# Holding side products back in the plan of a two-layer decoder trunk on one core

## The chip, the core and the metric

The kernel runs on one core of a Trainium2 chip. What counts is the device time of one execution in microseconds (us). Before the change three runs gave 1103.56, 1106.44 and 1106.52 us, the median is 1106.44. The engines are named PE (TensorE), ACT (ScalarE), DVE (VectorE), POOL (GpSimd) and SP (SyncE); SP and POOL also issue the DMAs.

## What is computed

Two layers of a decoder trunk take 256 prompt tokens and 8 sample tokens (264 columns) of width 2048. In each layer the input is normalised and projected by `w_in` into 57 column tiles of 128, three branches work on parts of that, each branch is multiplied by a gate, and `w_out` brings the 2048 mixed channels back:

```
h = rms_norm(x, norm_w)
z = h @ w_in
y_a = rwkv_time_mix(z_a, ...)      # 12 heads x 64, delta-rule state, one step a token
y_b = attention_branch(z_b, ...)   # 12 heads x 64 in 3 groups, windows 128/512/2048, dilation 1/4/16
y_c = pool_branch(z_c, ...)        # causal means over 2, 4, 8, 16 tokens, then a linear map
y = x + concat(y_a, y_b, y_c) @ w_out
```

New states, the last rows and the new keys and values are outputs too.

## The kernel before

**Stream and side products.** The two projections are the stream. Weights come in as `raw` tiles of 512 KB (`load`, 512 rows by 256 columns); ACT rounds each into `hi`, DVE writes the rest into `lo`, and PE multiplies `hi` by `xh`, `hi` by `xl` and `lo` by `xh`, the two halves of the input (in `w_out` by `mh`/`ml`, `mb` and `mc`, the halves of the mixed channels). Every stream matmul has 264 columns and adds into a PSUM bank of the tag `acc` (3 banks). All else that PE does are side products: transposes (`tr`, L118), small fp32 matmuls and a few of the rounded type (`mm`, L115). They write into PSUM banks of the tag `a` (5 banks), which ACT or DVE empties.

**What a layer does in order.** `layer` projects the tiles in pairs and hands each `z` to a branch. The A branch (`a_lora`, `a_k`, `a_kdone`, `a_r`, `a_solve`, `a_v`, `a_chain`) shifts tokens, builds Gram matrices of 64-token chunks, inverts triangular ones (`invert`, four products), goes through four chunks in sequence (`chunk`, four PE bundles each: with `gs`, with `rt`, with `bt`, and the output one with `gs` and `ar`) and normalises (`group_norm`, transposes of `ots`). Its tiles live in the pool `apool`. The pool `lpool` of `late` opens once `apool` is empty. There `b_prompt` does the banded attention of the prompt (scores, softmax, transposes, values), `b_sample` that of the 8 sample tokens against the caches (`rows`, `sc`, `sml`, `sev`, `ssm`, then for each of three groups `vc`, `ex`, `os`, `osb`), `c_u` the pooling. `b_mix` multiplies by the gates and writes `mb`. Then `w_out` runs; its first weights are multiplied by four `mb` channels (order 2, 1, 3, 0).

**The plan.** Written so, the program is only a set of instructions with dependences. `Plan` gives each a rough duration (`cost`), finds who needs whom (`dependences`), and `once` goes through time like a simulation: for each engine it takes the ready instruction of the highest priority and so writes the order in which that engine runs its instructions on the chip. Each engine then runs its list strictly in order and waits on semaphores where an operand isn't there. Priority (`prio`) is the longest tail of work behind an instruction (`tails`), and the first `lead` = 25 stream matmuls and what stands before them keep program order.

The parts of `once` that matter here:

- An instruction becomes ready when the planned ends of all whom it needs have passed, plus a fixed hop between engines (`HOP`), plus `slack` of the one that waits if the two stand on different engines or the first is a DMA. `slack` is `margin` for all, and 0 for stream matmuls and what feeds them.
- A PSUM or SBUF buffer is free again 100 to 150 ns behind the planned end of its last reader (`release`); `slack` isn't added there.
- PE has two heaps, stream (`PE`) and side products (`SIDE`). If a side product is ready and `go` holds, it is taken. `go` holds if a side product was the last taken (`side_on`), if the oldest has been ready for `wait`, or if the durations of those in the heap reach `batch`. If no stream matmul is ready a side product is taken anyway.
- Going from side products back to the stream is charged `switch` = 105 ns, the other way half of it for those that aren't in a bundle (`claims`).
- Products within `with self.bundle(...)` go one after another without a break (`forced`); only the first of a bundle stands in the heap.

Of the kernel before, what the change touches and what calls it, by code (L numbers as in the profile page):

```python
# [103 lines left out]
class Trunk:  # L104
# [1185 lines left out]
    def run(self):  # L1290
        self.setup()
        with self.tc.tile_pool(name="init", bufs=1, reuse_waits="tile") as ip:
            self.ip, self.early, self.xin = ip, [], []
            calm = ip.tile([P, T], F32, name="calm")
            self.nc.vector.memset(calm, 0.0)
            pt = self.ps("a")
            calmr = ip.tile([P, 512], F32R, name="calmr")
            self.nc.vector.memset(calmr.bitcast(F32), 0.0)
            for _ in range(8):
                self.mm(pt[:, :T], calm[:, :P], calm)  # L1300
            pu = self.ps("a")
            for n, outs, rows in ((T, (pt,), (slice(0, P),)), (T, (pt, pu), (slice(0, P),)), (256, (pt,), (slice(0, P),)),
                                  (512, (pu,), (slice(0, P),)), (P, (pt,), (slice(0, P),)), (T, (pt, pu), UROWS)):
                for i in range(5):
                    r = rows[i % len(rows)]
                    self.mm(outs[i % len(outs)][:, :n], calmr[r, :P], calmr[r, :n])
            self.act(ip.tile([P, 1], F32, name="table"), calm[:, 0:1], AF.Tanh)
            self.params(0)
            for c in range(4):
                x = ip.tile([P, 4, T], F32, tag="xin", name=self.nm("xin"), bufs=4)  # L1310
                self.dma(x, self.ins["x_cm"][4 * c:4 * c + 4].rearrange("k p t -> p k t"))
                self.xin.append(x)
                if c < 3:
                    self.early.append(self.load(self.ins["w_in"][0], 23 * P, 2 * P, c))
            self.accs = self.stream(self.ins["w_in"][0], 23 * P, 2, None, None, begin=True)
            self.dma(self.cbase, self.ins["cbase"])
            self.first_scale()
            self.more_params(0)
        for l in range(self.depth):
            self.layer(l)  # L1320
# [15 lines left out]
class Plan:  # L1336
# [200 lines left out]
                tail[q] = max(tail[q], t)  # L1537
        return tail

    def run(self, factor=1, hop=300, margin=200, batch=0, wait=0, switch=0, quiet=0, lead=1, dyn=(), ahead=0):  # L1540

        self.hold = [0.0] * self.n
        args = factor, hop, margin, batch, wait, switch, quiet, lead, dyn
        if ahead:
            self.once(*args)
            for k, i in enumerate(self.ins):
                if self.dma[k] and not self.feeds(k):
                    self.hold[k] = max(0.0, min([self.start[q] for q in self.after_load[k]], default=0.0) - ahead)
        return self.once(*args)
# [1 line left out]
    def feeds(self, k):  # L1551
        return self.tag[self.first_out[k]].startswith("raw") if self.first_out[k] in self.tag else False

    def once(self, factor, hop, margin, batch, wait, switch, quiet, lead, dyn):
        n, eng, preds, dma, dur, stream = self.n, self.eng, self.preds, self.dma, self.dur, self.stream
        spare = {t: d for t, r in self.ring.items() for m, d in dyn if t.split("_" + self.pool[r[0]])[0] == m}
        tail = self.tails(factor, hop, spare)
        head = [k for k in range(n) if stream[k]][lead - 1]
        prio = [k - 3e9 if k < head else -tail[k] for k in range(n)]
        feeds = {q for k in range(n) if stream[k] for q in preds[k]}  # L1560
        slack = [0 if stream[k] or k in feeds else margin for k in range(n)]
        bust = [self.bus(i) if d else 0 for i, d in zip(self.ins, dma)]
        succ = [[] for _ in range(n)]
        count = [0] * n
# [51 lines left out]
        def take(h):  # L1616
            while h:
                p, k = heapq.heappop(h)
                w = blocked(k)
                if w is None:  # L1620
                    return k
                parked[w].append(k)
            return None
# [5 lines left out]
        while done < n:  # L1629
            while pending and pending[0][0] <= now + 1e-9:  # L1630
                _, k = heapq.heappop(pending)
# [8 lines left out]
            for e in free:  # L1640
                if free[e] > now + 1e-9 or (e == "SP" and hw > now + 700):
                    continue
                if e == "PE" and forced is not None:
                    k = forced
                elif e == "PE":
# [3 lines left out]
                    k = None  # L1649
                    if h:  # L1650
                        go = side_on or h[0][0] < -2e9 or now - since >= wait or sum(dur[x[1]] for x in h) >= batch
                        if go:
                            k = take(h)
# [3 lines left out]
                    if k is None:  # L1657
                        k = take(ready["PE"])
                        if k is None and h:
                            k = take(h)  # L1660
# [3 lines left out]
                else:  # L1664
                    k = take(ready[e])
# [134 lines left out]
def build(nc, shapes, depth=DEPTH):  # L1800
    ins = {n: nc.dram_tensor(f"in_{n}", s, F32, kind="ExternalInput").ap() for n, s in shapes.items()}
    outs = {n: nc.dram_tensor(f"out_{n}", s, F32, kind="ExternalOutput").ap() for n, s in _OUTS}
    with tile.TileContext(nc, schedule_with_timeline_sim=True) as tc, ExitStack() as ctx:
        trunk = Trunk(ctx, tc, ins, outs, depth)
        trunk.run()
        plan = Plan(tc, trunk.bundles)
        plan.run(ahead=12000, switch=105, margin=350, hop=180, factor=0.9, lead=25, quiet=60, dyn=[("a", 2)])
        plan.apply()


# [10 lines left out]
```

## Time and profile before

| | before |
|---|---|
| median of three runs | 1106.44 us |
| the profiled execution | 1103.8 us |
| its span, first to last instruction | 1102.0 us |
| mean granted TensorE clock | 0.982 of 2.4 GHz |
| busy: PE, DVE, ACT, POOL | 1053.9, 857.2, 546.1, 133.6 us |
| stream of layer 0: `w_in`, `w_out` | 11 to 458 us, 458 to 551 us |
| stream of layer 1: `w_in`, `w_out` | 551 to 1005 us, 1005 to 1099 us |

A row of the timeline gives start and duration in us, engine, line, operation, the tiles (written, then read), the shapes, and how many instructions were merged; in brackets the idle time before and who ended it. Matmuls overlap, so a matmul's duration is longer than its distance to the next; distances are taken from start to start. A row of waits says who waited for whom, for how long in sum, how often, and the longest. In a table of stretches each row gives a stretch, its length and each engine's busy time with its number of instructions, then the granted clock and the DMA engines' share and rate.

### The profile page before, as it was taken

The numbers are of one execution on the slowest core, as the hardware profiler recorded it, in microseconds if no ns is written. First come the engines' busy times: TensorE is split into PE (matmuls) and PEld (weight loads), VectorE is DVE, ScalarE is ACT, GpSimd is POOL, SyncE is SP. The second block draws the span as 40 slices with busy tenths as digits, with TensorE's granted clock in tenths as the row PEclk, the third lists the DMA queues.
The fourth block names the chain that finished last, engine by engine and source line by source line (L and its number), as shares of the span: only waits on it lengthen the run. The fifth ranks groups of instructions, "written<-read, shape, count | busy, mean of one in ns | idle before, by whom it ended". The sixth has DMA issues, their size and how long they took to land.

```text
span 1102.0 us, 24574 instructions
## 1 busy us (share of the span) xinstructions
PE 1053.9 (96%) x9802; PEld 1004.4 (91%) x9802; DVE 857.2 (78%) x1684; ACT 546.1 (50%) x934; POOL 133.6 (12%) x262
## 2 busy tenths in 40 slices
PE   9999998989999998999999999989899998999998
PEld 8999898978999887999999988988899988879998
DVE  7769968979998887666675898768899869886443
ACT  7646433445645554454464563443466553744332
POOL 0004200200022100010010141001001111000000
PEclk9999999989999999999999999989999989999999
DMA  8654578886368855677765446878864568555774
GB/s 275 209 166 135 151 232 234 243 225 208 116 209 256 267 188 174 197 225 223 231 216 169 154 136 207 226 228 212 230 196 138 172 216 307 167 187 187 226 226 151
DMA packets 154683, 223.64 MB, mean 203 GB/s; under 512 B 75984, under 2 KB 109152, under 8 KB 154552
## 3 DMA queue, kind: packets, MB, share of 16 engines
q1 hardware_dynamic: 146456, 195.94, 58.7%
q0 software_dynamic: 8112, 26.12, 7.2%
q8 instruction: 77, 1.26, 0.5%
q14 instruction: 38, 0.31, 0.1%
HBM read 198.55 MB, written 24.03 MB: 202 GB/s over the span
## 4 chain that ended last, share of the span: by engine, by line
PE 58%; DVE 19%; DMA 12%; issue 5%; ACT 4%; SPq 1%; POOL 0%; DVEq 0%; ACTq 0%; POOLq 0%
PE acc L323 50%; DVE lo L140 6%; PE a L115 5%; DMA raw<-in_w_in 5%; PE a L118 2%; ACT hi L137 2%; DVE s L140 1%; DMA qb<-q_dram 1%; DVE z L140 1%; DMA vc<-in_cache_v_w 1%; SPq L155 1%; DVE bk L149 1%; DMA iv<-rb_dram 1%; ACT uv L137 1%; DVE bk L140 1%
## 5 line engine op out<-in xcount | busy, mean ns | idle before, releaser
L137 ACT ACTIVATE hi<-raw 128x1024 fp32r<-128x1024 f32 (+1 forms) x296 | 309.9, 1047 | 385.7 <-PE acc L323 257.6
L323 PE MATMUL acc<-xh,hi 128*128 128x264 f32 x1824 | 477.5, 291 | 4.3 <-ACT hi L137 3.0
L323 PE MATMUL acc<-xl,hi 128*128 128x264 f32 x1824 | 475.4, 291 | 0.2 <-DVE xl L149 0.2
L140 DVE TENSOR_TENSOR lo<-raw,hi 128x1024 fp32r<-128x1024 f32 (+1 forms) x296 | 357.1, 1207 | 137.2 <-ACT hi L137 135.3
L323 PEld LDWEIGHTS acc<-xh,hi 128*128 128x128 f32 x1824 | 348.2, 191 | 8.9 <-ACT hi L137 3.4
L323 PEld LDWEIGHTS acc<-xl,hi 128*128 128x128 f32 x1824 | 348.5, 191 | 6.2 <-issue 4.5
L323 PE MATMUL acc<-xh,lo 128*128 128x264 f32 x1824 | 300.7, 291 | 2.3 <-DVE lo L140 2.1
L323 PEld LDWEIGHTS acc<-xh,lo 128*128 128x128 f32 x1824 | 252.5, 191 | 9.7 <-issue 4.0
L140 DVE TENSOR_TENSOR z<-acc,rstd 128x264 f32<-128x264 f32 (+1 forms) x112 | 52.1, 466 | 25.0 <-PE acc L323 23.6
L323 PE MATMUL acc<-mb,hi 128*128 128x264 f32 x384 | 57.3, 284 | 0.2 <-DVE xs L140 0.2
L323 PEld LDWEIGHTS acc<-mb,hi 128*128 128x128 f32 x384 | 51.0, 188 | 0.5 <-DVE xs L140 0.5
L323 PE MATMUL acc<-mh,hi 128*128 128x264 f32 x192 | 49.3, 284 | 0.0
L323 PE MATMUL acc<-ml,hi 128*128 128x264 f32 x192 | 49.2, 284 | 0.0
L353 POOL COPY zcol<-z 128x9 f32<-128x9 f32 x50 | 19.4, 387 | 207.8 <-DVE z L140 193.9
L323 PEld LDWEIGHTS acc<-ml,hi 128*128 128x128 f32 x192 | 36.1, 188 | 0.0
L323 PEld LDWEIGHTS acc<-mh,hi 128*128 128x128 f32 x192 | 36.1, 188 | 0.0
L323 PE MATMUL acc<-mb,lo 128*128 128x264 f32 x192 | 33.8, 285 | 0.0
L323 PE MATMUL acc<-mc,hi 128*128 128x264 f32 x256 | 33.6, 284 | 0.0
L323 PE MATMUL acc<-mh,lo 128*128 128x264 f32 x192 | 33.6, 283 | 0.0
L140 DVE TENSOR_TENSOR xs<-acc,res 128x264 f32<-128x264 f32 x32 | 13.9, 433 | 24.3 <-DMA res<-resid 16.6
L323 PEld LDWEIGHTS acc<-mc,hi 128*128 128x128 f32 x256 | 32.1, 188 | 0.0
L323 PEld LDWEIGHTS acc<-mh,lo 128*128 128x128 f32 x192 | 27.6, 188 | 0.0
(357 smaller groups left out, 1309.7 us busy)
## 6 DMA issues: line engine op xcount, KB each, us to landing
raw<-in_w_in SPq DMA_DIRECT2D x224, 512.0 KB
raw<-in_w_out SPq DMA_DIRECT2D x64, 512.0 KB
g_dram<-gs SPq DMA_DIRECT2D x8, 768.0 KB
gs<-g_dram SPq DMA_DIRECT2D x8, 768.0 KB
kc<-in_cache_k_w POOLq DMA_DIRECT2D x12, 512.0 KB, 7.2
qb<-q_dram SPq DMA_DIRECT2D x12, 512.0 KB
vc<-in_cache_v_w POOLq DMA_DIRECT2D x12, 512.0 KB, 5.0
s<-in_state_wkv POOLq DMA_DIRECT2D x12, 256.0 KB, 5.0
```

Source lines behind the costliest of these rows:

```text
L115: self.note(self.nc.tensor.matmul(out, lhsT, rhs, start=start, stop=stop))
L118: self.note(self.nc.tensor.transpose(out, in_, self.c("ident")[base:base + k, base:base + k]))
L137: self.nc.scalar.activation(out, in_, func, **kw)
L140: self.nc.vector.tensor_tensor(out, a, b, op=op)
L149: self.nc.vector.scalar_tensor_tensor(out, a, s, b, op0=op0, op1=op1)
L155: self.nc.sync.dma_start(out, in_)
L323: self.nc.tensor.matmul(accs[t][:, :T], a[:, k4, cs], b[k], start=first, stop=q == order[3] and k4 == 3 and late == 1)
L353: self.nc.gpsimd.tensor_copy(self.zcol[:, :, a], z[:, NP - 1:T])
```

## The change

Three numbers of the planner's call change, and one is new. `margin` goes from 350 to 200 ns. `care` is new, 1200 ns: it takes the place of `margin` in `slack` for instructions on PE that are neither stream matmuls nor feed them (its default, which the call overrides, is 350). `batch` goes from 0 to 400 ns and `wait` from 0 to 1500 ns; with both at 0 `go` always held. Nothing is changed in what is computed.

```diff
-    def run(self, factor=1, hop=300, margin=200, batch=0, wait=0, switch=0, quiet=0, lead=1, dyn=(), ahead=0):
+    def run(self, factor=1, hop=300, margin=200, batch=0, wait=0, switch=0, quiet=0, lead=1, dyn=(), ahead=0, care=350):
...
-        args = factor, hop, margin, batch, wait, switch, quiet, lead, dyn
+        args = factor, hop, margin, batch, wait, switch, quiet, lead, dyn, care
...
-    def once(self, factor, hop, margin, batch, wait, switch, quiet, lead, dyn):
+    def once(self, factor, hop, margin, batch, wait, switch, quiet, lead, dyn, care):
...
-        slack = [0 if stream[k] or k in feeds else margin for k in range(n)]
+        slack = [0 if stream[k] or k in feeds else care if eng[k] == "PE" else margin for k in range(n)]
...
-        plan.run(ahead=12000, switch=105, margin=350, hop=180, factor=0.9, lead=25, quiet=60, dyn=[("a", 2)])
+        plan.run(ahead=12000, care=1200, batch=400, wait=1500, switch=105, margin=200, hop=180, factor=0.9, lead=25, quiet=60, dyn=[("a", 2)])
```

## Rows read from the trace of the kernel before

**Rows 1.** The page's first part: busy us, share of the span, instructions.

```profile
PE 1053.9 (96%) x9802; PEld 1004.4 (91%) x9802; DVE 857.2 (78%) x1684; ACT 546.1 (50%) x934; POOL 133.6 (12%) x262
```

**Rows 2.** Three stretches of layer 0: behind the chunks, attention, `w_out`.

```profile
296.00:316.00 20.00, 20.00 (x168) 19.99 (x167) 20.00 (x53) 9.30 (x14) 2.87 (x5) 1.00 0.59 178
316.00:405.00 89.00, 87.93 (x712) 81.57 (x709) 78.89 (x194) 53.19 (x127) 15.93 (x34) 0.98 0.75 237
...
458.00:551.00 93.00, 93.00 (x769) 93.00 (x768) 59.22 (x82) 46.38 (x66) 7.92 (x15) 1.00 0.72 225
```

**Rows 3.** PE's waits: in total us, times, longest us.

```profile
PE a L115 <- DMA vc<-in_cache_v_w: 3.4, 2, 1.9
PE acc L323 <- ACT hi L137: 3.0, 2, 1.8
PE a L115 <- ACT pt L137: 2.7, 2, 1.8
...
PE a L118 <- DVE ev L140: 0.5, 1, 0.5
...
PE a L115 <- ACT bt L137: 0.3, 1, 0.3
...
PE acc L323 <- DVE xs L140: 0.2, 1, 0.2
```

**Rows 4.** Stretches at half clock, stream matmuls alone: PE, PEld, clock; one, and eight summed.

```profile
428.30:431.70 3.40, 3.40 (x17) 3.40 (x17) 0.50 0.01 6
...
sum 37.70, PE 26.61 PEld 25.41; mean PE 3.33 PEld 3.18
```

**Rows 5.** Timeline of PE where side products stand in the stream.

```profile
27.36 0.63 PE L115 MATMUL a<-cbase,sqa 128*128 128x1 f32 x6
...
246.23 0.53 PE L323 MATMUL acc<-xh,lo 128*128 128x264 f32 x3
246.69 0.92 PE L115 MATMUL a<-uv,bt 128*64 128x64 f32 x24
247.44 0.87 PE L115 MATMUL a<-uv,gs 128*64 128x64 f32 x24
...
248.46 0.29 PE L323 MATMUL acc<-xl,hi 128*128 128x264 f32 x1
...
280.57 0.28 PE L323 MATMUL acc<-xl,hi 128*128 128x264 f32 x1
280.79 0.92 PE L115 MATMUL a<-uv,gs 128*64 128x64 f32 x24
...
281.86 0.28 PE L323 MATMUL acc<-xl,hi 128*128 128x264 f32 x1
...
371.23 0.28 PE L323 MATMUL acc<-xl,hi 128*128 128x264 f32 x1
371.35 0.60 PE L118 MATMUL a<-cbase,tok 128*128 128x128 f32 x4
...
371.91 0.28 PE L323 MATMUL acc<-xl,hi 128*128 128x264 f32 x1
...
985.32 0.29 PE L323 MATMUL acc<-xh,hi 128*128 128x264 f32 x1
985.45 0.38 PE L118 MATMUL a<-cbase,os 128*128 128x128 f32 x2
...
985.79 0.29 PE L323 MATMUL acc<-xh,hi 128*128 128x264 f32 x1
```

**Rows 6.** Timeline: the last halves of `mb`, the first matmuls that take `mb`.

```profile
439.71 0.77 DVE L140 TENSOR_TENSOR mb<-sgb,mb 128x264 fp32r<-128x264 f32 x2
...
458.05 0.53 PE L323 MATMUL acc<-mb,hi 128*128 128x264 f32 x3
...
988.77 0.77 DVE L140 TENSOR_TENSOR mb<-sgb,mb 128x264 fp32r<-128x264 f32 x2
...
1004.77 0.53 PE L323 MATMUL acc<-mb,hi 128*128 128x264 f32 x3
```

## The prediction

> **What bounds the kernel now.** The page comes first. PE is busy in 96% of the 1102.0 us span [rows 1]. The second view is the stretches: the output projection of layer 0 is nothing but stream, 768 matmuls in 93.00 us, 0.121 us each [rows 2]. The kernel has 7008 such matmuls (5472 into `w_in`'s tiles, 57 x 16 x 3 x 2 layers, and 1536 for `w_out`), so 848 us are a floor that the change can't touch. The other 254 us are side products, PE's waits, and time at half clock.
>
> Third, the list of PE's waits [rows 3], which is to be read by who is waited for; each of the three kinds stands there with its first and its last row. In fifteen of the rows a side product waits for an operand (a DMA, or a step of ACT, DVE or POOL that makes its input): vc 3.4, os 2.7, z 2.6, x 2.5, comp 2.5, 1.1 and 1.0, cd 2.1, right 1.2, compb 1.0, iv 0.9, nwt 0.9, dg 0.7, p 0.7, ev 0.5, in sum 23.8 us in 23 waits. In eight rows it waits until an earlier step has emptied the PSUM bank that it wants (ACT pt, uv, u, u and bt, DVE zv, kk and st): 7.2 us. The stream itself waits only 6.0 us in five rows (`hi` 3.0, `lo` 2.1, `z` 0.5, `xl` and `xs` 0.2 each). As PE takes its queue in order, each of these holds up the stream behind it. They are the plan's misjudgements: it put the side product in PE's queue where it thought the operand would have been there for 0.35 us.
>
> Fourth, the granted clock. Eight stretches, 37.7 us together, ran at the lower level, 1.2 GHz of 2.4, as the one from 428.3 does right behind the longer wait for `vc` [rows 3, 4].
>
> **The change, part by part.** No instruction is added or taken away and no semaphore is new; the queues' orders alone move.
>
> *More room before side products (margin 0.35 to 1.20 us).* Each operand wait may shrink by 0.85 us, no more. Row by row that is the smaller of the row's total and 0.85 times its count: 1.7 (vc), 1.7, 2.55, 0.85, 1.7, 1.1, 1.0, 1.7, 0.85, 0.85, 0.85, 0.85, 0.7, 0.7, 0.5, in sum 17.6 us [rows 3]. I take 17. The bounds are 0 (the new order only meets other late steps) and 23.8 us (small products are held longer still). Waits for a bank don't get the margin: the planner frees a bank at the planned end of its reader, and that isn't padded. New orders bring new lateness. I put that at 5 us, between 0 and 10, by its nearest rows: 7.2 us for banks and 6.0 us of the stream.
>
> *The clock.* In the eight slow stretches 120 stream matmuls kept PE busy for 26.61 us, where 0.121 each gives 14.5: 12.1 us lost [rows 2, 4]. Half of the eight stand behind operand waits; the one behind `vc` lost 3.40 - 17 x 0.121 = 1.3 us. I take a quarter back, 3 us; bounds 0 and 12.
>
> *Waiting for company (400 ns of queued work, or 1.5 us).* The plan charges 105 ns for going back to the stream and half of that for leaving it. What the chip charges is seen by counting from one stream matmul to another across a stretch. From 985.32 to 985.79 lie two stream matmuls (one before and one behind) and two transposes: 0.47 less 2 x 0.121 is 0.23 us. From 371.23 to 371.91 lie two and four: 0.68 less 0.24 is 0.44 [rows 5]. That is 0.11 us a transpose whether two or four go together, so joining transposes is worth nothing. Bundles of small fp32 matmuls differ: 24 alone take 280.57 to 281.86 less two stream matmuls, 1.05 us; 48 in one stretch take 246.23 to 248.46 less four, 1.75 [rows 5]. Joining two saves 2 x 1.05 - 1.75 = 0.35 us. The program has 74 such bundles (32 in the chunks, 12 Gram, 12 score, 12 value, 6 of squares). Those of a chunk follow from one another and can't meet, and the ones with a common operand already stand together. I count a dozen joinings, 4 us; bounds a loss of 2 (a transpose that joins a bundle has no row here; 0.02 us each way for a hundred) and a gain of 37 x 0.35 = 13.
>
> *What the delays do to the chain behind them.* A side product put later makes its eviction on ACT or DVE late, and all that follows. The long chain of a layer is: four products of the inversion, three bundles in each of four chunks, the transposes of `ots`, then (the pool `lpool` opens only when `apool` is empty) in `b_sample` five small transposes and three rounds of values and transposes: 28 steps on PE. Each costs 0.85 more, less 0.15 for each of some three steps of ACT, DVE, POOL and DMA between (margin 0.35 to 0.20): net 0.4, so 11 us. Twenty of them queue less than 400 ns (a bundle counts only its first matmul) and may be held up to 1.5 us; at half of that, 15 us. So 26 us a layer if all of it lies on the path. The end of the path is the last `mb` half that `w_out` wants first. It is ready at 440.48 and wanted at 458.05, 17.6 us later; in layer 1 at 989.54 and 1004.77, 15.2 us [rows 6]. What speaks for cover: the chain now waits for DVE, not for PE. DVE is busy in 20.00 of 20 us behind the chunks and in 78.89 of 89 in the attention that follows [rows 2]. A step that comes later to a full queue loses less than its delay. With half covered, 13 us arrive and the slack takes them. I charge 2 us in all, bounds 0 (`w_out` starts without a wait already, so nothing is to be gained) and 49 (below).
>
> *Less room for the others (0.35 to 0.20).* Late inputs hold ACT's and DVE's queues, behind which `hi` and `lo` stand; the stream waits 3.0 and 2.1 us for those now [rows 3]. I add 2 us, bounds -2 (earlier evictions) and 5 (twice today's). SP's and POOL's stores are planned 0.15 us earlier, of no weight; the raw loads wait for buffers, which get no margin.
>
> The sum: -17 - 3 - 4 + 5 + 2 + 2 = -15 us on the 1102.0 us span, 1087. That execution took 1103.8 us and the median of the three runs is 1106.44, so I set the change against the median: 1091.
>
> A rule against this: the Trainium skill (Perfetto Trace Analysis, Optimization Strategy) says that consistent bubbles on the engine that should be full can mean too little SBUF or PSUM for the next tile. By it the waits would be for banks and a margin on operands would give nothing, about 1106. The trace splits against it, 23.8 us for operands and 7.2 for banks [rows 3].
>
> **The rivals.** *The chain becomes the bound (slower).* If DVE doesn't cover, each layer's `w_out` starts late by the chain's growth less its slack. At 26 us: 8.4 + 10.8 = 19 us; with every hold at its full 1.5 us, 41 us a layer: 23 + 26 = 49, of which 2 are in the sum. The result is -15 + 17 = +2 to +32; at a hold of 1.1 us (33 us a layer) stalls of 15 + 18 and +16: 1122. It is slower from a growth of some 27 us on. For it: the planner ranks steps by a tail that knows neither the new margin nor the pool that must close, so it won't hurry this chain. Against: the full DVE queue, and 1.5 us pass only where no other side product is queued.
>
> *The waits only move.* Banks asked for by several products at once take the place of operands; PE's waits stay near 44 us: 1106. Two such waits (ACT pt) already cost 2.7 us [rows 3].
>
> *The plan's price for switches is right.* 231 stretches of side products stand in the stream (the first, of `sqa`, at 27.36, the last, of `os`, at 985.45 [rows 5]). If half go, each at 0.157 us, 18 us instead of 4: 1077. Against it stand the transposes, at no price.
>
> **How the numbers follow.** Forecast 0.55 (alone 1083 to 1101), late chain 0.22, waits move 0.13, dear switches 0.10. About 0.3% (3.3 us) is what a measurement of this kernel can tell from no change. Faster by that: 0.53 + 0.10 + 0.01 = 0.64; within: 0.02 + 0.10 + 0.02 = 0.14; slower: 0.02 of moved waits and 0.20 of the late chain = 0.22. The range 1076 to 1118 leaves out the worse half of the late chain and a sliver below.
>
> **What would show it.** Right: side products' operand waits fall from 23.8 to some 7 us, slow-clock stretches to half, the first `mb` matmul comes earlier than 458 and 1004.8 with no wait before it. Wrong: a wait of the stream for `mb` or `mh` at `w_out`'s start (late chain); bank waits of over 12 us (waits move); far fewer stretches and a stream less interrupted by more than the waits explain (dear switches). I would be wrong most simply if the new order's own late steps are as many as the old one's.

## The result, and the profile after

The changed kernel took 1089.17 us (median of five runs, 1085.48 to 1096.22); the kernel before, beside it, 1103.73 (1101.6 to 1106.52). The ratio is 0.9874, with a 95% interval of 0.984 to 0.9908; by the medians it is 14.6 us faster. (A run over 1.5% above the fastest of its kernel is left out of medians and ratios below; this befell one, the profiled run of company alone.) The profiled execution took 1087.3 us, its span 1085.5, against 1103.8 and 1102.0.

The line of the page for the kernel after that answers to [rows 1]:

```profile
PE 1045.3 (96%) x9802; PEld 997.2 (92%) x9802; DVE 856.8 (79%) x1684; ACT 546.3 (50%) x934; POOL 136.3 (13%) x262
```

The same 9802 matmuls keep PE busy 8.6 us less; the other 7.9 us of the span are PE's empty time, which fell from 48.1 to 40.2. Where that lies is read from the stretches (length, then PE, PEld, DVE, ACT and POOL with their instructions, the granted clock, the DMA engines). First the two `w_in` streams of the kernel before, for which the rows above give only parts:

```profile
10.84:458.05 447.21, 427.15 (x4112) 403.48 (x4111) 377.34 (x777) 233.50 (x421) 61.88 (x116) 0.98 0.67 203
551.20:1004.77 453.57, 430.10 (x4112) 406.33 (x4111) 368.93 (x758) 226.69 (x407) 61.13 (x123) 0.97 0.65 197
```

Then all four streams of the kernel after:

```profile
11.39:457.46 446.07, 425.44 (x4111) 402.19 (x4111) 377.85 (x778) 233.70 (x420) 59.30 (x116) 0.99 0.68 203
457.46:550.67 93.21, 93.21 (x770) 93.21 (x769) 59.08 (x82) 46.24 (x65) 8.14 (x15) 1.00 0.74 225
550.67:988.07 437.40, 422.49 (x4112) 400.04 (x4111) 368.71 (x759) 226.59 (x408) 66.50 (x122) 0.99 0.68 204
988.07:1082.30 94.23, 93.90 (x770) 93.30 (x768) 45.69 (x53) 33.60 (x34) 0.00 (x0) 1.00 0.66 206
```

`w_out` is as long as it was [rows 2]. In this execution nearly all of the gain is in layer 1's `w_in`: 453.57 to 437.40 us, 16.2 less, against 1.1 in layer 0. The mean granted clock of both rose (0.98 to 0.99 and 0.97 to 0.99).

PE's waits after (in total us, times, longest us), to be held against [rows 3]:

```profile
PE a L115 <- DMA rat<-rat_dram: 3.7, 1, 3.7
PE a L115 <- DMA vc<-in_cache_v_w: 3.4, 3, 1.7
PE acc L323 <- DVE z L140: 3.3, 3, 1.6
PE acc L323 <- ACT hi L137: 2.9, 4, 1.3
PE a L115 <- ACT pt L137: 2.7, 1, 2.7
PE a L115 <- issue: 2.6, 1, 2.6
```

Sorted as the prediction sorted them (all rows over 0.15 us, summed by kind), before and after: operands of side products 23.7 and 14.0 us, banks 7.2 and 8.9, the stream's own tiles 6.0 and 8.5, "issue" 5.8 and 2.7. With 1.2 us at the start in each, 43.9 and 35.3. `vc` costs as much as before in three waits instead of two. `rat` is new at the top. `pt` has the 2.7 us that it had in [rows 3], but there they were two waits for a bank, and here it is one wait of a product for `pt` itself. The sorting isn't sharp: a few rows name a tile that the waiting product doesn't read (`compb` and `nwt` before, `s` after, some 2 us in each), and they could as well be counted as banks.

The stretches at half clock, stream matmuls alone, as in [rows 4], are five now instead of eight:

```profile
43.70:47.10 3.40, 3.40 (x18) 3.40 (x17) 0.50 0.15 10
217.80:221.20 3.40, 3.40 (x18) 3.40 (x17) 0.50 1.39 236
350.90:354.30 3.40, 1.78 (x8) 1.85 (x8) 0.50 0.89 297
767.30:770.70 3.40, 2.64 (x13) 2.33 (x11) 0.50 1.16 308
975.50:978.90 3.40, 3.40 (x18) 3.40 (x17) 0.50 0.58 174
sum 17.00, PE 14.62 PEld 14.38; mean PE 2.92 PEld 2.88
```

75 stream matmuls take 14.62 us there; at 0.121 each they would take 9.1. So 5.5 us are lost, 12.1 before. What stands ahead of each is in PE's timeline (in brackets the idle time and who ended it):

```profile
42.37 0.39 PE L323 MATMUL acc<-xh,hi 128*128 128x264 f32 x1 [1.63 <-DVE z L140]
...
216.20 1.31 PE L115 MATMUL a<-rat,x 32*32 32x16 f32 x96 [3.68 <-DMA rat<-rat_dram]
...
350.77 1.05 PE L115 MATMUL a<-pt,tok 128*64 128x128 f32 x8 [2.74 <-ACT pt L137]
...
765.47 1.17 PE L115 MATMUL a<-iv,x 32*32 32x32 f32 x96 [2.18 <-DVE s L140]
...
974.20 0.64 PE L115 MATMUL a<-vc,ppad 128*32 128x256 f32 x8 [1.72 <-DMA vc<-in_cache_v_w]
```

Each of the five slow stretches begins within two microseconds of the end of a wait of 1.63 to 3.68 us: such a wait looks to be paid for twice, though no run set a wait on its own. Not every one is: no slow stretch follows the "issue" wait of 2.6 us.

Last, the end of the path, as in [rows 6]: the last halves of `mb` and the first matmuls that take them.

```profile
439.01 0.77 DVE L140 TENSOR_TENSOR mb<-sgb,mb 128x264 fp32r<-128x264 f32 x2
...
457.46 0.53 PE L323 MATMUL acc<-mb,hi 128*128 128x264 f32 x3
...
984.53 0.78 DVE L140 TENSOR_TENSOR mb<-sgb,mb 128x264 fp32r<-128x264 f32 x2 [0.41 <-ACT mb L137]
...
988.07 0.41 PE L323 MATMUL acc<-mb,hi 128*128 128x264 f32 x2
```

In layer 1 the tile is ready at 985.31 and wanted at 988.07: 2.8 us ahead instead of 15.2. In layer 0 it is 17.7, as before (17.6). This lead of the last `mb` over the stream is called the slack below (it has nothing to do with `slack` in the plan).

### The profile page after: what moved, and what is told of

Its sections match the earlier page's. It is cut to its first block, busy times and chain, and to the rows that moved or that the text cites. A ratio compares the mean times of both kernels' runs of the same rounds, so it can differ in the third digit from the quotient of the medians.

```text
span 1085.5 us, 24558 instructions
## 1 busy us (share of the span) xinstructions
PE 1045.3 (96%) x9802; PEld 997.2 (92%) x9802; DVE 856.8 (79%) x1684; ACT 546.3 (50%) x934; POOL 136.3 (13%) x262
## 4 chain that ended last, share of the span: by engine, by line
PE 53%; DVE 23%; DMA 12%; issue 5%; ACT 5%; SPq 1%; DVEq 0%; ACTq 0%; POOLq 0%
PE acc L323 46%; DVE lo L140 7%; PE a L115 6%; DMA raw<-in_w_in 3%; DMA qb<-q_dram 2%; ACT hi L137 2%; PE a L118 2%; DVE z L140 2%; SPq L155 1%; DVE tm L140 1%; DMA svec<-sk_dram 1%; DVE s L140 1%; DMA rwkv_a_up<-in_rwkv_a_up 1%; DMA res<-resid 1%; DMA q_dram<-brows 1%
## 5 line engine op out<-in xcount | busy, mean ns | idle before, releaser
L323 PE MATMUL acc<-xh,lo 128*128 128x264 f32 x1824 | 295.6, 289 | 2.3 <-DVE lo L140 2.1
L323 PEld LDWEIGHTS acc<-xh,lo 128*128 128x128 f32 x1824 | 249.9, 190 | 8.1 <-DVE lo L140 3.9
```

The costliest lines, as they stand in the source:

```text
L323: self.nc.tensor.matmul(accs[t][:, :T], a[:, k4, cs], b[k], start=first, stop=q == order[3] and k4 == 3 and late == 1)
```

## The experiments

The change turns four numbers at once: `care`, the room before a side product (0.35 to 1.20 us), `margin` for the other engines (0.35 to 0.20), and `batch` with `wait`, the holding back for company. Theory: the gain is `care`'s, through fewer waits for operands and less time at half clock. Rivals: it is company's, through fewer switches; or any new order would have done it. Each edit is to the planner's call of the changed kernel, shown as far as it differs. In short, `care` is called room, and `batch` with `wait` company. Waits, half-clock time and slack are read from one profiled execution of each kernel, as above; ratios are against runs of the kernel before that were taken beside it.

### Each part alone

*Room alone.*

```diff
-plan.run(ahead=12000, care=1200, batch=400, wait=1500, switch=105, margin=200, ...
+plan.run(ahead=12000, care=1200, margin=350, switch=105, ...
```

> Only the room before side products grows (care 1200; margin 350, batch 0 and wait 0 as before). Theory: the gain of the whole change comes from operand waits that the room takes away: about 1092 us (-12), operand waits of side products near 9 us instead of 23.8, about 231 stretches of side products as before. Rival 1 (the gain is fewer switches): 1104 us, no change. Rival 2 (any new order gains or loses some us by chance): anywhere from 1095 to 1110, with operand waits not tied to it.

Measured: 1080.91 us (1079.32 to 1087.98), ratio 0.9821 [0.9765, 0.9876]. It gives the whole gain and, by its median, more. The profiled execution is the slowest of its four, 1087.98 us, about the changed kernel's 1087.3, so its waits can't show where the lower median comes from. The longest of them:

```profile
PE a L115 <- issue: 5.7, 4, 3.3
PE acc L323 <- ACT hi L137: 5.1, 3, 2.8
PE a L115 <- DMA rat<-rat_dram: 2.8, 1, 2.8
PE acc L323 <- DVE z L140: 2.7, 3, 1.6
PE a L115 <- DVE cd L140: 2.0, 1, 2.0
```

Two of these five rows are the stream's own (`acc`), two are operands of side products; `vc`, the longest operand wait in [rows 3] with 3.4 us, is down to 1.8. Operand waits are 11.7 us in all (23.7 before), 20.5 us ran at half clock (37.7), and the slack ahead of `w_out` is 17.2 us in both layers. 221 stretches of side products stand in the stream, 231 before: ten fewer, 1.6 us at the plan's price of 0.157 each, so the gain is not a matter of switches.

*The shorter margin alone.*

```diff
+plan.run(ahead=12000, care=350, margin=200, switch=105, ...
```

> Only the room before steps of the other engines shrinks (margin 200, care 350, batch 0 and wait 0). Theory: PE's operand waits stay near 24 us, more late hi and lo: 1104 to 1108 us (0 to +4). Rival 1: 1104 us. Rival 2: 1095 to 1110. If it is faster by over 5 us, shorter chains were worth more than the 2 us that the prediction charged the other way.

Measured: 1098.0 us (1094.29 to 1104.89), ratio 0.9956 [0.9925, 0.9986]. Operand waits stay at 22.2 us and half-clock time at 41.0. Slightly faster, where the prediction had charged 2 us.

*Company alone.*

```diff
+plan.run(ahead=12000, care=350, margin=350, batch=400, wait=1500, switch=105, ...
```

> Only the waiting for company (batch 400, wait 1500; care and margin 350). Theory: a dozen joined bundles save 4 us, and the hold takes some of the operand waits with it (23.8 to some 17 us): 1094 to 1100 us. Rival 1 (switches are worth what the plan says): 1089 us with under 200 stretches. Rival 2: 1095 to 1110.

Measured: 1087.56 us (1084.58 to 1090.39), ratio 0.9868 [0.981, 0.9926]. This came as a surprise. The profiled execution is the one left out, of 1100.91 us at a granted clock of 0.984, and doesn't show where the gain of the three others came from: operand waits 19.4 us, half-clock time 34.1. Of what the order alone sets it shows 192 stretches instead of 231, slack of 15.6 and 14.1 us.

*Room and the shorter margin, without company.*

```diff
+plan.run(ahead=12000, care=1200, margin=200, switch=105, ...
```

> Room of 1200 for side products and 200 for the others, no waiting for company (batch 0, wait 0). Theory: 1092 to 1094 us, about 4 us over the whole change, operand waits near 9 us, about 231 stretches. Rival 1: 1104 us. Rival 2: 1085 to 1105.

Measured: 1095.31 us (1092.1 to 1099.99), ratio 0.9948 [0.9917, 0.9978]. In this order the shorter margin seems to take back most of what room alone gave. Operand waits are 19.5 us despite the room of 1.2 us. One product alone waits 3.4 us for `vc`: it was misplaced by far more than any of these numbers, which a change of a number can bring about by chance. So the next question was how much chance there is.

### How much of it is the chance of one order

Each kernel was built again with one of its numbers moved a little (10 to 100 ns), which makes another order of the same intent.

*Before, jogged.*

```diff
+plan.run(ahead=12000, care=360, margin=360, switch=105, ...
```

> A jog of the kernel before: margin 360 and care 360 instead of 350, nothing else. 10 ns should mean nothing by themselves, but the orders come out different in many places. Theory (operand waits and the clock set the time): within 5 us of the kernel before (1102), operand waits 18 to 26 us. Rival (any new order moves the time by as much as the parts did): 1085 to 1095 us, or over 1108.

Measured: 1102.76 us (1098.05 to 1104.81), ratio 0.9983 [0.9965, 1.0001]. This one new order gives nothing; other orders can still come out by chance, as the next ones show.

*Room alone, jogged.*

```diff
+plan.run(ahead=12000, care=1100, margin=350, switch=105, ...
```

> A jog of the room alone: care 1100 instead of 1200 with margin 350, no waiting for company. Theory: as with 1200, which measured 0.982 of the kernel before: 1080 to 1088 us, operand waits 9 to 13 us. Rival (the gain with 1200 was a lucky order): 1090 to 1105 us with operand waits as low all the same.

Measured: 1084.54 us (1082.16 to 1085.66), ratio 0.9828 [0.9806, 0.985]. It holds. The first of its waits:

```profile
PE a L115 <- issue: 8.6, 5, 3.9
PE acc L323 <- ACT hi L137: 3.8, 4, 1.4
```

Operand waits are down to 7.6 us, the fewest of all; half-clock time is 23.9. The largest row is no operand: before products such as that of `iv` and `y` PE stood without a semaphore that it waited for (the last section tells what the trace shows of it).

*Room and shorter margin, jogged.*

```diff
+plan.run(ahead=12000, care=1100, margin=200, switch=105, ...
```

> A jog of room and shorter margin together: care 1100 instead of 1200, margin 200, no waiting for company. Theory (a shorter margin for the other engines costs beside more room, since their queues then hold up more often): 1092 to 1098 us, as with 1200 (0.995 of the kernel before). Rival (0.995 was one unlucky order, the margin costs nothing): 1080 to 1088 us.

Measured: 1086.65 us (1082.96 to 1088.54), ratio 0.9824 [0.9767, 0.9882]. The loss of `care_margin` is gone with a 100 ns jog, so it was that one order's and not the shorter margin's.

*Company alone, jogged.*

```diff
+plan.run(ahead=12000, care=350, margin=350, batch=400, wait=1400, switch=105, ...
```

> A jog of waiting for company alone: batch 400, wait 1400 instead of 1500, care and margin 350. Theory (the hold is worth something by itself, as room and by some 40 fewer stretches): 1085 to 1093 us, operand waits 14 to 19 us, under 200 stretches. Rival (0.987 was one lucky order): 1096 to 1106 us.

Measured: 1095.32 us (1093.26 to 1099.31), ratio 0.9932 [0.9903, 0.9961], half of what the first company kernel gave, and between the range of the theory and that of the rival. Its first waits:

```profile
PE a L115 <- issue: 9.1, 4, 3.1
PE a L115 <- DMA vc<-in_cache_v_w: 7.7, 2, 5.2
```

Operand waits 18.9 us, 190 stretches. The side stretches, summed by counting from stream matmul to stream matmul, took some 4 us less than before's. That is the most that 41 fewer stretches are worth, since less of them ran at half clock, too.

### Does company add to room?

```diff
+plan.run(ahead=12000, care=1200, margin=350, batch=400, wait=1500, switch=105, ...
```

> Room of 1200 and waiting for company, with margin 350 as before; the whole change but for the shorter margin of the other engines. Theory: the shorter margin only costs, as it did beside the room alone (0.995 with it, 0.982 without): 1075 to 1083 us. Rival (room and company take the same waits, so don't add): 1081 to 1089 us. Rival (order by chance): up to 1100 us.

Measured: 1089.72 us (1086.24 to 1095.17), ratio 0.9882 [0.9843, 0.992]. This is the change without its shorter margin, and the time is the same (0.9874). Against room alone nothing is gained, and the time lies above the range of the theory. Waiting for company is also a delay between an operand and its product, so both may take the same waits (operands 10.9 us here, 11.7 with room alone); one order doesn't show it. In layer 1 the slack shrinks to 8.9 us.

### How much room is right, and when the chain becomes the bound

*Three times the room.*

```diff
+plan.run(ahead=12000, care=3600, margin=350, switch=105, ...
```

> Room of 3600 for side products, margin 350, no company. Theory: operand waits near 4 us, but 28 steps a layer come 2.4 us later than with 1200, up to 67 us a layer; what DVE doesn't cover stops the stream before w_out (slack now 17 us): waits of the stream over 20 us, 1100 to 1140 us. Rival (the chain is covered by DVE's queue however long): 1075 to 1085 us.

Measured: 1124.25 us (1123.17 to 1126.82), ratio 1.0194 [1.0174, 1.0213]. This is the prediction's rival of the late chain, made to happen. Operand waits did not fall to near 4 us, as expected, but rose to 27.5. The two `w_out` streams of it:

```profile
469.57:572.14 102.57, 99.22 (x787) 96.66 (x787) 59.52 (x84) 45.82 (x65) 8.17 (x15) 0.94 0.64 197
1015.24:1117.50 102.26, 98.90 (x782) 96.34 (x783) 47.09 (x55) 33.14 (x34) 0.00 (x0) 0.94 0.60 181
```

102.57 and 102.26 us instead of 93.2 and 94.2. PE's timeline, and then DVE's, at the start of the first:

```profile
469.57 1.50 PE L323 MATMUL acc<-mb,hi 128*128 128x264 f32 x5 [1.10 <-ACT mb L137]
...
476.30 0.69 PE L118 MATMUL a<-cbase,os 128*128 128x128 f32 x2 [2.26 <-ACT os L137]
...
478.08 1.72 PE L323 MATMUL acc<-mb,hi 128*128 128x264 f32 x6 [1.09 <-ACT mb L137]
```

```profile
478.06 0.78 DVE L140 TENSOR_TENSOR mb<-sgb,mb 128x264 fp32r<-128x264 f32 x2 [0.41 <-ACT mb L137]
```

The transposes of `os`, steps of the chain, still run 6.7 us after `w_out` began, and the last half of `mb` is ready 9.3 us after that start. With nothing left to fill the queue, PE waits for the chain:

```profile
PE a L118 <- ACT os L137: 13.5, 6, 3.1
PE acc L323 <- DVE lo L140: 11.3, 8, 4.8
PE acc L323 <- DVE z L140: 8.5, 6, 2.3
```

The stream's own waits rose as well, from 6.0 us before to 30.8.

*Between the two.*

```diff
+plan.run(ahead=12000, care=2000, margin=350, switch=105, ...
```

> Room of 2000 for side products, margin 350, no company: between 1200 (0.982) and 3600 (1.019). Theory (the chain of layer 1 has some 17 us left at 1200 and grows by up to 28 x 0.8 = 22 us, half of it covered): the stream doesn't yet wait for mb, operand waits 3 to 7 us, 1076 to 1084 us. Rival (the growth isn't covered): mb comes after w_out's turn, 5 us late in each layer, 1086 to 1096 us.

Measured: 1092.86 us (1090.65 to 1096.11), ratio 0.9894 [0.9843, 0.9944]. The median is higher than with 1.2 us, above the range of the theory, but the chain doesn't stop the stream: the last `mb` is ready 3.5 us before it is wanted (DVE's timeline, then PE's).

```profile
456.88 1.00 DVE L140 TENSOR_TENSOR mb<-sgb,mb 128x264 fp32r<-128x264 f32 x2
```

```profile
461.34 0.89 PE L323 MATMUL acc<-mb,hi 128*128 128x264 f32 x6
```

Operand waits (10.5 us) are no fewer than at 1.2, half-clock time is a mere 3.4 us, but waits for banks are 13.6 us and those of the stream 13.3; `w_in` of layer 0 ended at 461.3 us, with 1.2 at 451.5. In this order too much room costs banks and late stream tiles before it costs a stop at `w_out`. It is one order, and its interval overlaps that of 1.2 us.

*More margin beside the room.*

```diff
+plan.run(ahead=12000, care=1200, margin=500, switch=105, ...
```

> Room of 1200 for side products and 500 instead of 350 for the other engines, no company. Theory (room for the other engines saves waits of their queues, as the shorter margin lost them): 1074 to 1081 us. Rival (350 is enough, and 80 more steps a layer at 0.15 us each eat the slack of the chain): 1081 to 1090 us, slack before w_out under 10 us.

Measured: 1090.94 us (1085.37 to 1096.21), ratio 0.9873 [0.9808, 0.9939]. Operand waits 12.1 us, slack 11.9 and 6.0: no better than a margin of 0.35, by its median 10 us worse, with intervals that overlap. The range of the theory is missed.

Side by side, with waits and half-clock time in us:

| kernel | ratio | operands | banks | stream | half clock | slack, layers 0 and 1 |
|---|---|---|---|---|---|---|
| before | 1 | 23.7 | 7.2 | 6.0 | 37.7 | 17.6, 15.2 |
| after | 0.987 | 14.0 | 8.9 | 8.5 | 17.0 | 17.7, 2.8 |
| room 1.2 | 0.982 | 11.7 | 6.4 | 8.5 | 20.5 | 17.2, 17.2 |
| room 1.1 | 0.983 | 7.6 | 6.0 | 5.8 | 23.9 | 14.9, 17.7 |
| room 2.0 | 0.989 | 10.5 | 13.6 | 13.3 | 3.4 | 3.5, 2.8 |
| room 3.6 | 1.019 | 27.5 | 5.2 | 30.8 | 58.0 | late, late |
| company, jogged | 0.993 | 18.9 | 7.9 | 6.3 | 30.7 | 15.1, 15.1 |
| room and company | 0.988 | 10.9 | 7.9 | 11.3 | 10.2 | 15.3, 8.9 |

Room alone, at 1080.9 us, has the lowest median of all, below both kernels, and its jogged twin at 1084.5 is the next lowest; against the changed kernel's 0.984 to 0.9908 their intervals (0.9765 to 0.9876 and 0.9806 to 0.985) overlap, so that they beat it is likely, not shown.

## Why the prediction was right

The forecast was 1091 us, 15 below the median of before; measured were 1089.17 and a fall of 14.6. By the profiled executions it was 16.5. The mechanism is the one that was named. The terms were not all of the right size, and that the sum came out within 1 us is luck in part: room gave 7.3 us less than its 17, the clock 3.6 more than its 3, 3.1 came from "issue" waits that no term had, and the 4 charged for the chain and the margin can't be seen. The measured parts add up to 19 us (9.7 of operands, 6.6 of the clock, some 4 of joining and 3.1 of "issue", less 4.2 of lateness), 2.7 more than the execution gained, so some of them overlap or something stays uncounted.

- **What bounds the kernel**: right. The stream's floor did not move (`w_out` 93 us in both), and the gain lies where PE waited and where it ran at half clock.
- **Room, -17 us less 5 of new lateness**: the mechanism is right, the size too large. Operand waits fell by 9.7 us, from 23.7 to 14.0, net of new ones; the two terms together forecast 12. The step that was mis-sized is the row-by-row rule that a wait shrinks by 0.85 us each: it takes the old waits to be the only ones. A new order has its own: `rat` 3.7 us and the wait of 2.7 us for `pt` as an operand were not in the list of before. As a sign of being right some 7 us were named; it was 14.0. Room alone came to 11.7 and 7.6 us, so the 17 was not out of reach without company. The lateness, put at 5 us, shows as 1.7 for banks and 2.5 for the stream, 4.2 in sum; the stream's part answers to the 2 us charged to the shorter margin, too.
- **The clock, -3 us**: too small. 6.6 us came back (12.1 lost before, 5.5 after). The prediction took back a quarter; there are five slow stretches now where eight were, with 17.0 us in place of 37.7.
- **Joining, -4 us**: as forecast in size. Stretches of side products went from 231 to 196, and their time fell by about 4 us (an estimate: 7 in all, less what half clock had cost them). PE's timeline after shows the price of a joining. Alone, then joined:

```profile
114.06 0.90 PE L323 MATMUL acc<-xh,lo 128*128 128x264 f32 x6
114.89 0.32 PE L115 MATMUL a<-cbase,comp 64*48 64x64 f32 x4
115.14 0.51 PE L323 MATMUL acc<-xh,lo 128*128 128x264 f32 x2
115.48 0.28 PE L323 MATMUL acc<-xh,hi 128*128 128x264 f32 x1
...
117.43 1.00 PE L323 MATMUL acc<-xh,lo 128*128 128x264 f32 x7
118.36 0.43 PE L115 MATMUL a<-cbase,comp 64*48 64x64 f32 x8
118.72 0.39 PE L323 MATMUL acc<-xh,lo 128*128 128x264 f32 x1
118.95 0.28 PE L323 MATMUL acc<-xh,hi 128*128 128x264 f32 x1
```

  From the first row's start to the last's lie 1.42 us with eight stream matmuls (0.97), so four small products cost 0.45; eight cost 1.52 - 0.97 = 0.55. Two joined save 0.35, the price the prediction read from [rows 5]. Transposes joined to no saving, as forecast: two take 0.23 us, four 0.44, in the kernel after as well (medians of 27 and 15 stretches). Beside enough room, these 4 us are not seen in the time.
- **The chain, +2 us**: right in its result. It arrives 12.4 us later against the stream in layer 1 (slack 15.2 to 2.8), where 13 was forecast. But the agreement is partly by another road: the end of the chain came 4.2 us earlier (its last row from 988.77 to 984.53), while the stream came 16.7 earlier (1004.77 to 988.07). The estimate spoke of a chain that grows; it fell behind because the stream ran away from it. In layer 0 the reading of [rows 6] was wrong: that slack is 17 to 18 us in seven of the fourteen kernels, because the last `mb` there waits for the stream's own gate tiles, finished a fixed number of matmuls before `w_out` (before, the last gate is written to `sgb` at 436.67 us, 3.0 ahead of the last `mb`). It told nothing of the chain until the chain grew past that point, as with 2.0 us of room.
- **Margin for the others, +2 us**: not shown. Alone it was a little faster (0.9956), with room and company no difference (0.9874 and 0.9882), with room 0.995 in one order and 0.982 in another. Its own effect is below what an order's chance does.
- **Not foreseen**: 3.1 us less of "issue" waits, which other kernels here have at anything from 0 to 10.9. They look to be waits for PE's own instructions (last section), and no part of the change aims at them.

Of the rivals, the **late chain** is real but begins elsewhere: with 3.6 us of room (and no company) `w_out` stalled by 9 us a layer and the time was 1124.25. That this is near the rival's 1122 is chance, since the 1122 was for the whole change with another delay. With room of 1.2 us alone the stop is 17 us off, with 2.0 some 3, and in the changed kernel, which has company and the shorter margin beside its 1.2, only 2.8 in layer 1. **The waits only move** fell: PE's waits went from 43.9 to 35.3 us where they would have stayed near 44, though it describes what 2.0 us of room does (banks 7.2 to 13.6). **Dear switches** fell as to their number: half of 231 were to go, and 35 to 41 went, worth 5.5 to 6.4 us at the plan's 0.157 each, where some 4 came. That the price is no fixed one shows in the transposes, at 0.11 us each whether two or four stand together.

Three things stay open. How company alone gained 1.3% in its first order and 0.7% in the second isn't shown, since none of the first's three counted executions was profiled. Room gives the whole gain without company; that company had no part in the changed kernel's own gain is not shown. Why one order with room and the shorter margin lost 9 us to its jogged twin (1095.31 and 1086.65) was not followed further than its longer operand waits (19.5 and 16.1 us). And that the gain was all in layer 1 is this execution's: the first two kernels with room ended layer 0's `w_in` at 451.5 and 453.5 us, up to 6.5 us earlier than before, without company.

## What to carry to other kernels

Where one engine takes its work in a fixed order and other work stands in it, a late operand stops everything behind it; put the product later than the plan's estimate says, by about the length of the waits that the trace shows (here 1 us for waits of 0.5 to 2), and look at the granted clock for a second part of the gain. Measure the slack of the longest chain first, and stop well before it is used up: 1.1 to 1.2 us gave 1.7 to 1.8%, 2.0 gave 1.1% (in one order), 3.6 lost 1.9%. Before a number of a planner is praised or blamed for some 1%, move it by a trifle and measure again: another order of the same intent moved the time by up to 9 us.

## What was not expected of the hardware

The half-clock rows after a wait: in the kernel after all five slow stretches of 3.4 us stand behind waits of 1.6 to 3.7 us, and of 37.7 us at half clock in the kernel before a third was lost time (12.1 us). With 2.0 us of room only 3.4 us ran at half clock, and yet the kernel was no faster than with 1.2: the clock is only one part.

PE stood for up to 3.9 us at the products of `iv` and `y` with no semaphore to wait for in the profile, in several kernels and in the middle of a product (these rows are from room alone, jogged):

```profile
225.90 0.45 PE L115 MATMUL a<-iv,y 32*32 32x32 f32 x31
230.28 1.11 PE L115 MATMUL a<-iv,y 32*32 32x32 f32 x65 [3.94 <-issue]
```

The traces point to PE's own instructions, which come by DMA. The page has a queue for instructions (packets, MB, share of the DMA engines) whose count fits PE:

```profile
q8 instruction: 77, 1.26, 0.5%
```

77 packets of 16 KB for PE's 19604 matmuls and weight loads are one packet for about 256 instructions. Of the 44 "issue" waits in the fourteen kernels, 40 (72.0 of 75.4 us, and all 21 of over 2 us) end at the same place, give or take one, when PE's instructions are counted in blocks of 256, each 1.2 to 1.7 us after the end of a packet of this queue. Above, the packet ran from 227.85 to 228.90 us, and PE went on at 230.28. The stream, at 0.121 us for a matmul and its load, takes 15 us for 256 instructions (an estimate); 96 of the small matmuls take 1.17 (the row at 765.47 above), with as many loads, so several such products close together may use up their instructions faster than the packets come. No experiment moved these waits on purpose. With 0 to 10.9 us a kernel they can be as large as the waits for operands, and the plan knows nothing of them.

A transpose of 128 x 128 costs 0.11 us whether two or four stand together, while in the two cases read here (24 and 48 products, 4 and 8) a bundle of small products has a fixed part of 0.35 us that joining saves.
